# Head pairs on halves of the matrix array, and a router that searches two rows in turn

## The chip, the cores and the metric

The kernel runs on one core of a Trainium2 chip. The metric is the device time of one execution in microseconds (us). TensorE (PE in the profile, its weight loads PEld) multiplies, VectorE (DVE) and ScalarE (ACT) work elementwise and reduce, GpSimd (POOL) helps with a few elementwise jobs, and SyncE (SP) issues the transfers that bring weights from HBM.

## The reference, cut to what matters

One sequence of 256 rows and width 1024 goes through a pool mixer, a feed-forward block, chunk attention, a second feed-forward block, a block with two branches (retention and stick-breaking attention), and PEER, an expert layer. Four pieces matter here.

```python
# chunk attention, 16 heads of 64 (scores q.k, bias, mask, softmax, values)
s = jnp.einsum('bqhd,bkhd->bhqk', qc, kb) * scale + bias[None]
p = jax.nn.softmax(jnp.where(valid, s, -1e30), axis=-1)
o = jnp.einsum('bhqk,bkhd->bqhd', p, vb)          # then o @ w_o
# stick-breaking, 8 heads of 64
z = jnp.einsum('bhtd,bhsd->bhts', qi, kh) * scale
later = lax.cumsum(log_stay, axis=3, reverse=True) - log_stay
w = jnp.where(mask, jnp.exp(jax.nn.log_sigmoid(z) + later), 0.0)
out = jnp.einsum('bhts,bhsd->bhtd', w, vh)
# retention, 8 heads with q and k of 64, v of 128
scores = jnp.einsum('bihd,bjhd->bhij', qc, kc) * dmask[None]
# PEER: 16 of 128 sub-keys twice, then 16 of their 256 sums, for each row and head
v1, i1 = lax.top_k(s1, 16); v2, i2 = lax.top_k(s2, 16)
top_s, pos = lax.top_k(v1[..., :, None] + v2[..., None, :], 16)
a = gelu(u_tab[idx] @ x) * softmax(top_s)         # and y = sum of a * v_tab[idx]
```

## The kernel before, in words

All activations stay on the chip; rows are two blocks (b = 0, 1) of 128 partitions. Weights stream from HBM as slabs. Each slab is split into a rounded high part (`whi`, ScalarE, L72) and the rest (`wlo`, VectorE, L80 or L86, a few on GpSimd), and `mm3` (L107 to L111) makes each product of three matmuls. Outside PEER, a planner orders the instructions of each engine from estimated costs, and so fills TensorE with projections (`acc`) while heads wait for other engines. PSUM has four `acc` tiles, three `w` tiles and one `o` tile; `w` tiles are handed out in program order.

**Attention** (`attention`, L443). `qkv(g)` projects eight heads, `heads(g, h0)` works on four of them, head by head: `weights` (scores of 64 rows of the array by L480 and L481, bias L484, maxima L486, exponentials L487 with their sums), `turn` (three transposes L494 and a copy L496) and `values` (L501 to L503: the stationary operand is the turned weights, 128 by 128, the moving one v, 64 columns). After four heads the sum's reciprocal (L515) scales the `o` tile (L517), and `transposed` (L206) turns it again into `oT`, the operand of `out_proj`. Attention calls `heads` four times; the projection of the second half of the heads, and then `out_proj`, lie around them.

**Stick-breaking** (L577) has the same shape: `stay` (L606, L607 and five elementwise instructions), `weights` (L622 to L630), `values` (L636 to L638), a copy and four transposes for four heads. Its two calls are placed between the projections of **retention** (L661), whose `heads` computes scores by L709 and L710 one head at a time.

**PEER** (`peer`, L747) is ordered by hand for TensorE, VectorE and ScalarE. In eight steps `h` it projects the queries (`qps`, L793), computes sub-key scores (`scores`, L968), and in steps 1 and 2 transposes the normalized input into `hn` through `w` and `o` tiles (L801). Then 128 expert slabs follow: `up(i)` (L822, 24 matmuls into `hps`) needs `whi` and `wlo` of slab i. The **router** (`route`, L983) is a generator: each step issues some VectorE work and yields its cost in units; `side(rout, upto)` runs it until the units spent reach `upto`. In step h that is `5 h`, and in the slab loop

```python
for i in range(N1):
    self.prefetch(3, later=True)          # whi of slab i + 2 on ScalarE
    if not side(rout, 36 + i * 1.6):      # router's work on VectorE
        last = i; break
    self.lows()                           # wlo of slab i + 2 on VectorE
    up(i)
```

so that VectorE runs two slabs ahead of TensorE, behind the router's steps. `top16` (L1083) finds 16 maxima of a row by five instructions, each of which needs the one before (MAX8, FIND_INDEX8, MATCH_REPLACE8, MAX8, FIND_INDEX8; the match ones are preceded by a MATCH_VALUE_LOAD). It runs 32 times on 128 columns and 16 times on 64. When the router is done (slab `last`), one-hot matrices for 64 groups of four rows are spread over the other slabs, and the second half of PEER follows.

Of the kernel before, what the change touches and what calls it, by code (L numbers as in the profile page):

```python
# [8 lines left out]
F32 = mybir.dt.float32  # L9
# [4 lines left out]
AF = mybir.ActivationFunctionType  # L14
OP = mybir.AluOpType
# [4 lines left out]
S = 256  # L20
# [26 lines left out]
class K:  # L47
# [158 lines left out]
    def transposed(self, hi, lo, src, b, kts, gcol=None, k0=0):  # L206
# [236 lines left out]
    def attention(self):  # L443
# [27 lines left out]
        def heads(g, h0):  # L471

            o = self.ps.tile([128, 2, 4, 64], F32, tag="o", name="o_ps", bufs=1)
            rs = self.small.tile([128, 2, 4], F32, tag="rsum", name="rsum")
            ss, ps = {}, {}

            def weights(h):
                p, hs = h // 2, slice((h % 2) * 64, (h % 2) * 64 + 64)
                sc = self.ps.tile([128, 384], F32, tag="w", name="sc", bufs=self.nw)
                nc.tensor.matmul(sc[:, 0:128], qT[g][hs, p, 0:128], kT[g][hs, p, 0:128], start=True, stop=True)  # L480
                nc.tensor.matmul(sc[:, 128:384], qT[g][hs, p, 128:256], kT[g][hs, p, :], start=True, stop=True)  # L481
                s = ss[h] = self.stage.tile([128, 384], F32, tag="s", name="s", bufs=3)
                m = self.small.tile([128, 2], F32, tag="mx", name="mx")
                nc.vector.tensor_tensor(s, sc, bias[g][:, h, :], op=OP.add)  # L484
                for b, c in ((0, slice(0, 128)), (1, slice(128, 384))):
                    nc.vector.tensor_reduce(m[:, b:b + 1], s[:, c], axis=AX.X, op=OP.max, negate=True)  # L486
                    nc.scalar.activation(s[:, c], s[:, c], AF.Exp, bias=m[:, b:b + 1],  # L487
                                         accum_out=rs[:, b, h - h0:h - h0 + 1])

            def turn(h):  # L490
                pt = self.ps.tile([128, 3, 128], F32, tag="w", name="pt_ps", bufs=self.nw)
                s = ss.pop(h)
                for j in range(3):
                    nc.tensor.transpose(pt[:, j], s[:, j * 128:(j + 1) * 128], self.ident)  # L494
                ps[h] = self.stage.tile([128, 3, 128], F32, tag="pT", name="pT", bufs=2)
                nc.scalar.activation(ps[h], pt, AF.Copy)  # L496

            def values(h):
                pT = ps.pop(h)
                v = [vv[g][:, b, h * 64:(h + 1) * 64] for b in range(2)]  # L500
                nc.tensor.matmul(o[:, 0, h - h0], pT[:, 0], v[0], start=True, stop=True)  # L501
                nc.tensor.matmul(o[:, 1, h - h0], pT[:, 1], v[0], start=True, stop=False)
                nc.tensor.matmul(o[:, 1, h - h0], pT[:, 2], v[1], start=False, stop=True)  # L503

            weights(h0)
            weights(h0 + 1)
            turn(h0)
            for h in range(h0, h0 + 4):
                if h + 2 < h0 + 4:
                    weights(h + 2)  # L510
                if h + 1 < h0 + 4:
                    turn(h + 1)
                values(h)
            ri = self.small.tile([128, 2, 4], F32, tag="rinv", name="rinv")
            nc.vector.reciprocal(ri, rs)  # L515
            on = self.stage.tile([128, 2, 4, 64], F32, tag="on", name="on", bufs=2)
            nc.vector.tensor_tensor(on.rearrange("p b h d -> p (b h) d"), o.rearrange("p b h d -> p (b h) d"),  # L517
                                    ri.rearrange("p b h -> p (b h)")[:, :, None].to_broadcast([128, 8, 64]),
                                    op=OP.mult)
            for b in range(2):  # L520
                self.transposed(oT[0], oT[1], on[:, b].rearrange("p h d -> p (h d)"), b, 2,
                                k0=g * 4 + h0 // 2)

        qkv(0)
        heads(0, 0)
        heads(0, 4)
        qkv(1)
        heads(1, 0)
        heads(1, 4)
        self.out_proj(lambda k: (oT[0][:, k], oT[1][:, k]))  # L530

# [45 lines left out]
    def stick_breaking(self, hT, r):  # L577
# [19 lines left out]
        def heads(h0):  # L597
            if h0 == 0:
                self.tc.keep_in_program_order(nc.scalar.preload_act_table_set("natural_log_exp_and_others"))
            o = self.ps.tile([128, 2, 4, 64], F32, tag="o", name="sbo", bufs=1)  # L600
            logs = {}

            def stay(h):
                p, hs = h // 2, slice((h % 2) * 64, (h % 2) * 64 + 64)
                z = self.ps.tile([128, 384], F32, tag="w", name="z", bufs=self.nw)
                nc.tensor.matmul(z[:, 0:256], kT[hs, p, 0:128], qT[hs, p, :], start=True, stop=True)  # L606
                nc.tensor.matmul(z[:, 256:384], kT[hs, p, 128:256], qT[hs, p, 128:256], start=True, stop=True)  # L607
                a = st.tile([128, 384], F32, tag="sb_a", name="sb_a", bufs=3)
                sp = st.tile([128, 384], F32, tag="sb_sp", name="sb_sp", bufs=3)
                logs[h] = a, sp  # L610
                nc.scalar.activation(a, z, AF.Abs)
                nc.scalar.activation(a, a, AF.Exp, scale=-1.0)
                nc.scalar.activation(a, a, AF.Ln, bias=1.0)
                nc.vector.scalar_tensor_tensor(sp, z, 0.0, a, op0=OP.max, op1=OP.add)
                nc.vector.scalar_tensor_tensor(a, z, 0.0, a, op0=OP.min, op1=OP.subtract)
                for c in (0, 256):
                    self.strictly_before(sp[:, c:c + 128])

            def weights(h):
                a, sp = logs[h]  # L620
                lt = self.ps.tile([128, 384], F32, tag="w", name="lt", bufs=self.nw)
                nc.tensor.matmul(lt[:, 0:256], self.tri, sp[:, 0:256], start=True, stop=False,  # L622
                                 skip_group_check=True)
                nc.tensor.matmul(lt[:, 128:256], self.ones, sp[:, 256:384], start=False, stop=True,
                                 skip_group_check=True)
                nc.tensor.matmul(lt[:, 256:384], self.tri, sp[:, 256:384], start=True, stop=True,
                                 skip_group_check=True)
                nc.vector.tensor_tensor(a, a, lt, op=OP.subtract)
                nc.scalar.activation(a, a, AF.Exp)
                for c in (0, 256):  # L630
                    self.strictly_before(a[:, c:c + 128])

            def values(h):
                a, _ = logs.pop(h)
                vh = [v[:, b, h * 64:(h + 1) * 64] for b in range(2)]
                nc.tensor.matmul(o[:, 0, h - h0], a[:, 0:128], vh[0], start=True, stop=True)  # L636
                nc.tensor.matmul(o[:, 1, h - h0], a[:, 128:256], vh[0], start=True, stop=False)
                nc.tensor.matmul(o[:, 1, h - h0], a[:, 256:384], vh[1], start=False, stop=True)  # L638

            stay(h0)  # L640
            for h in range(h0, h0 + 4):
                if h + 1 < h0 + 4:
                    stay(h + 1)
                weights(h)
                if h > h0:
                    values(h - 1)
            values(h0 + 3)
            on = st.tile([128, 2, 4, 64], F32, tag="yn", name="sbn", bufs=2)
            nc.scalar.activation(on, o, AF.Copy)
            for b in range(2):  # L650
                self.transposed(yT[0], yT[1], on[:, b].rearrange("p h d -> p (h d)"), b, 2, k0=h0 // 2)

        self.later = [lambda: heads(0), lambda: heads(4)]
# [7 lines left out]
    def retention(self, hT, r):  # L661
# [38 lines left out]
        def heads(h0):  # L700
            sc = st.tile([128, 4, 384], F32, tag="rsc", name="rsc", bufs=1)
            for j in range(4):
                h = h0 + j
                if j % 2 == 0:
                    dec = st.tile([128, 2, 384], F32, tag="dec", name="dec", bufs=1)
                    nc.sync.dma_start(dec, self.ins["c_decay"][:, h:h + 2])
                p, hs = h // 2, slice((h % 2) * 64, (h % 2) * 64 + 64)
                ps = self.ps.tile([128, 384], F32, tag="w", name="rs", bufs=self.nw)
                nc.tensor.matmul(ps[:, 0:256], kT[hs, p, 0:128], qT[hs, p, :], start=True, stop=True)  # L709
                nc.tensor.matmul(ps[:, 256:384], kT[hs, p, 128:256], qT[hs, p, 128:256], start=True, stop=True)  # L710
# [541 lines left out]
```

## Time and profile before

| | |
|---|---|
| median of 3 runs | 1604.07 us (1604.07 to 1605.76) |
| profiled execution | 1604.23 us, span 1602.5 us |
| mean granted TensorE clock | 0.995 |
| TensorE busy | 1565.4 us, 98% |
| TensorE weight loads busy | 1401.5 us, 87% |
| VectorE busy | 1160.3 us, 72% |
| ScalarE busy | 843.0 us, 53% |
| GpSimd busy | 105.0 us, 7% |

The span runs from the first to the last instruction of the program; 1.7 us of the execution lie around it. Busy shares are means over stages; matmuls are pipelined and their ends are modelled, so two matmuls overlap in the record, and the distance from start to start is what one costs the engine. A matmul of plain float32 operands shows as two records.

### The profile page before, as it was taken

What the parts mean: (1) busy time and instruction counts of PE and PEld (TensorE: products, weight loads), DVE (VectorE), ACT (ScalarE), POOL (GpSimd) and SP (SyncE); (2) the same over time, 40 slices, a digit from 0 to 9 for tenths busy, and PEclk for the clock granted to TensorE, in tenths of its full rate; (3) what the DMA queues carried; (4) which work ended last, traced back from release to release, by engine and by line L of the source; (5) the groups of instructions that cost most, each with busy time, mean ns of one, the idle gap of its engine ahead of it and who ended that gap; (6) DMA issues with size and microseconds to landing.
All of it is one profiled execution on the core that took longest, in us unless ns stands there. A gap on an engine that the chain in (4) does not pass through costs nothing.

```text
span 1602.5 us, 26447 instructions
## 1 busy us (share of the span) xinstructions
PE 1565.4 (98%) x10190; PEld 1401.5 (87%) x10190; DVE 1160.3 (72%) x2479; ACT 843.0 (53%) x1563; POOL 105.0 (7%) x111
## 2 busy tenths in 40 slices
PE   5999999999999999999999999999999999999999
PEld 4999987779999887888898999999999888888887
DVE  7676777767767877675599987788888655555554
ACT  6555565565555647444554555454444544454453
POOL 5000020010000202000260000000000000000000
PEclk9999999999999999999999999999999999999999
DMA  5555464325555552455424555555555666666664
GB/s 218 181 196 198 168 237 175 132 83 192 201 183 201 187 183 106 152 178 200 167 76 136 167 174 169 170 171 159 170 161 170 186 197 196 189 194 196 194 192 152
DMA packets 58446, 278.66 MB, mean 174 GB/s; under 512 B 6480, under 2 KB 7376, under 8 KB 41680
## 3 DMA queue, kind: packets, MB, share of 16 engines
q1 hardware_dynamic: 58320, 276.97, 52.6%
q8 instruction: 80, 1.31, 0.3%
q14 instruction: 46, 0.38, 0.1%
HBM read 275.90 MB, written 1.05 MB: 173 GB/s over the span
## 4 chain that ended last, share of the span: by engine, by line
PE 87%; DVE 9%; issue 2%; ACT 1%; DMA 1%; POOL 0%; SPq 0%; DVEq 0%; ACTq 0%; POOLq 0%
PE acc L110 15%; PE acc L111 15%; PE acc L109 15%; PE hps L109 6%; PE hps L111 6%; PE hps L110 6%; PE up L110 5%; PE up L111 5%; PE up L109 5%; PE gps L869 2%; DVE wlo L86 1%; DVE wlo L80 1%; DVE topk L1088 1%; DVE ix L1087 1%; DVE ix L1090 1%
## 5 line engine op out<-in xcount | busy, mean ns | idle before, releaser
L72 ACT ACTIVATE whi<-raw 128x512 fp32r<-128x512 f32 (+1 forms) x764 | 556.3, 769 | 381.3 <-PE acc L111 158.4
L80 DVE TENSOR_TENSOR wlo<-raw,whi 128x512 fp32r<-128x512 f32 (+1 forms) x572 | 448.6, 812 | 137.7 <-ACT whi L72 137.5
L111 PE MATMUL hps<-hn,wlo 128*128 128x256 f32 x1024 | 289.2, 282 | 8.6 <-DVE wlo L86 8.5
L109 PE MATMUL hps<-hn,whi 128*128 128x256 f32 x1024 | 293.5, 287 | 0.0
L110 PE MATMUL hps<-hn,whi 128*128 128x256 f32 x1024 | 287.1, 280 | 0.0
L111 PEld LDWEIGHTS hps<-hn,wlo 128*128 128x128 f32 x1024 | 194.0, 189 | 10.7 <-DVE wlo L86 10.6
L110 PE MATMUL up<-hT,whi 128*128 128x256 f32 x704 | 197.8, 281 | 1.5 <-DVE hT L223 1.5
L109 PE MATMUL up<-hT,whi 128*128 128x256 f32 x704 | 198.1, 281 | 0.4 <-DVE hT L223 0.4
L111 PE MATMUL up<-hT,wlo 128*128 128x256 f32 x704 | 197.4, 280 | 0.0
L110 PE MATMUL acc<-wlo,hn 128*128 128x512 f32 x504 | 196.2, 389 | 0.0
L111 PE MATMUL acc<-whi,hn 128*128 128x512 f32 x504 | 196.2, 389 | 0.0
L109 PE MATMUL acc<-whi,hn 128*128 128x512 f32 x504 | 196.2, 389 | 0.0
L110 PEld LDWEIGHTS hps<-hn,whi 128*128 128x128 f32 x1024 | 194.5, 190 | 0.0
L109 PEld LDWEIGHTS hps<-hn,whi 128*128 128x128 f32 x1024 | 194.3, 190 | 0.0
L86 DVE TENSOR_TENSOR wlo<-raw,whi 128x1024 fp32r<-128x1024 f32 x128 | 155.8, 1219 | 14.8 <-ACT whi L72 14.1
L110 PEld LDWEIGHTS up<-hT,whi 128*128 128x128 f32 x704 | 133.6, 190 | 3.3 <-DVE hT L223 2.0
L109 PEld LDWEIGHTS up<-hT,whi 128*128 128x128 f32 x704 | 133.5, 190 | 2.1 <-issue 0.7
L111 PEld LDWEIGHTS up<-hT,wlo 128*128 128x128 f32 x704 | 133.6, 190 | 0.0
L110 PE MATMUL acc<-wlo,hT 128*128 128x512 f32 (+1 forms) x320 | 125.0, 391 | 2.2 <-DVE wlo L80 1.2
L80 POOL TENSOR_TENSOR wlo<-raw,whi 128x512 fp32r<-128x512 f32 x64 | 84.3, 1347 | 636.0 <-ACT whi L72 629.3
L111 PE MATMUL acc<-whi,hT 128*128 128x512 f32 (+1 forms) x320 | 124.7, 390 | 0.0
L109 PE MATMUL acc<-whi,hT 128*128 128x512 f32 (+1 forms) x320 | 124.4, 390 | 0.0
(291 smaller groups left out, 2486.1 us busy)
## 6 DMA issues: line engine op xcount, KB each, us to landing
raw<-in_peer_u SPq DMA_DIRECT2D x128, 512.0 KB, 3.6
raw<-in_peer_v SPq DMA_DIRECT2D x128, 512.0 KB, 3.6
raw<-in_wup SPq DMA_DIRECT2D x44, 1024.0 KB, 4.9
raw<-in_win SPq DMA_DIRECT2D x26, 1024.0 KB, 4.8
raw<-in_wdn SPq DMA_DIRECT2D x22, 1024.0 KB, 4.8
raw<-in_wqkv SPq DMA_DIRECT2D x12, 1024.0 KB, 4.9
raw<-in_wo SPq DMA_DIRECT2D x8, 1024.0 KB, 4.8
raw<-in_peer_wq SPq DMA_DIRECT2D x8, 1024.0 KB, 4.8
```

The costliest lines, as they stand in the source:

```text
L72: i = nc.scalar.activation(hi[:, c:c + n], raw[:, c:c + n], AF.Copy)
L80: low(*args, op=OP.subtract)
L86: self.nc.vector.tensor_tensor(*self.low_parts.pop(0), op=OP.subtract)
L109: mm(ps, lh, rh, start=start, stop=False)
L110: mm(ps, lh, rl, start=False, stop=False)
L111: mm(ps, ll, rh, start=False, stop=stop)
L869: nc.tensor.matmul(ps[:, j], jh[:, j], gh[:, n, j], start=n == 0, stop=n == 1)
L1087: nc.vector.max_index(out=ix[:, 0:8], in_max=v[:, 0:8], in_values=s)
L1088: nc.vector.match_replace(out=t, in_to_replace=v[:, 0:8], in_values=s, imm_value=-3.0e38)
L1090: nc.vector.max_index(out=ix[:, 8:16], in_max=v[:, 8:16], in_values=t)
```

## The change

Heads are handled in pairs. The two heads of a pair lie on partitions 0 to 63 and 64 to 127 of the same q and k tile, so that their score matmuls use the two row halves of the array; the change issues them one behind the other. The values are computed transposed: v (64 columns) is the stationary operand, the weights the moving one, and the two heads write the two partition halves of one `o` tile of 128 by 256. So `oT` comes out of `split` directly; in attention the weights are normalized before they are turned. In the router, `top16` takes two rows and issues each of its five steps for both, and yields after the second step too; `unstair` is cut into three steps; some unit costs and the slope (1.6 to 1.5) change. The transposes of PEER's input go through `acc` tiles.

```diff
-            tag, bufs = ("o", 1) if kts == KT and b == 1 and k == 4 else ("w", self.nw)
+            tag, bufs = bank or (("o", 1) if kts == KT and b == 1 and k == 4 else ("w", self.nw))
...
-        def heads(g, h0):
+        def heads(g, pairs):
...
+            def weights(p):
+                sc = [self.ps.tile([128, 384], F32, tag="w", name="sc", bufs=self.nw) for _ in range(2)]
+                hs = [slice(e * 64, e * 64 + 64) for e in range(2)]
+                for e in range(2):
+                    nc.tensor.matmul(sc[e][:, 0:128], qT[g][hs[e], p, 0:128], kT[g][hs[e], p, 0:128],
+                                     start=True, stop=True)
+                for e in range(2):
+                    nc.tensor.matmul(sc[e][:, 128:384], qT[g][hs[e], p, 128:256], kT[g][hs[e], p, :],
+                                     start=True, stop=True)
+                s = ss[p] = self.stage.tile([128, 2, 384], F32, tag="s", name="s", bufs=2)
...
+                for e in range(2):
+                    nc.vector.tensor_tensor(s[:, e], sc[e], bias[g][:, 2 * p + e, :], op=OP.add)
+                    for b, c in parts:
+                        nc.vector.tensor_reduce(m[:, e, b:b + 1], s[:, e, c], axis=AX.X, op=OP.max, negate=True)
+                        nc.scalar.activation(s[:, e, c], s[:, e, c], AF.Exp, bias=m[:, e, b:b + 1],
+                                             accum_out=rs[:, e, b:b + 1])
+                nc.vector.reciprocal(ri, rs)
+                for e in range(2):
+                    for b, c in parts:
+                        nc.vector.tensor_scalar(s[:, e, c], s[:, e, c], ri[:, e, b:b + 1], None, op0=OP.mult)
...
+            def values(p):
+                pT = ps.pop(p)
+                o = self.ps.tile([128, S], F32, tag="o", name="o_ps", bufs=1)
+                self.head_values(o, [vv[g][:, b, p * 128:(p + 1) * 128] for b in range(2)],
+                                 [pT[:, e].rearrange("p j t -> p (j t)") for e in range(2)])
+                self.split(oT[0][:, g * 4 + p], oT[1][:, g * 4 + p], o)
+            last = None
+            for p in pairs:
+                weights(p)
+                if last is not None:
+                    values(last)
+                turn(p)
+                last = p
+            values(last)
...
+    def head_values(self, o, v, w):
+        mm = self.nc.tensor.matmul
+        for b in range(2):
+            for e in range(2):
+                hs = slice(e * 64, e * 64 + 64)
+                t = slice(b * 128, S)
+                c = slice(0, 256) if b == 0 else slice(256, 384)
+                mm(o[hs, t], v[b][:, hs], w[e][:, c], start=b == 0, stop=b == 1, skip_group_check=True)
...
-                    self.transposed(*hT, xn.pop(0), h - 1, KT, V_FFN2)
+                    self.transposed(*hT, xn.pop(0), h - 1, KT, V_FFN2, bank=("acc", 4))
...
-                if not side(rout, 36 + i * 1.6):
+                if not side(rout, 36 + i * 1.5):
...
+    def top16(self, rt, cost, rows):
+        vec = self.nc.vector
+        t = [rt.tile([128, 128], F32, tag="topk", name="topk", bufs=4)[:, :s.shape[1]] for _, _, s in rows]
+        for v, _, s in rows:
+            vec.max(out=v[:, 0:8], in_=s)
+        for v, ix, s in rows:
+            vec.max_index(out=ix[:, 0:8], in_max=v[:, 0:8], in_values=s)
+        yield cost
+        for (v, _, s), r in zip(rows, t):
+            vec.match_replace(out=r, in_to_replace=v[:, 0:8], in_values=s, imm_value=-3.0e38)
+        for (v, _, s), r in zip(rows, t):
+            vec.max(out=v[:, 8:16], in_=r)
+        for (v, ix, s), r in zip(rows, t):
+            vec.max_index(out=ix[:, 8:16], in_max=v[:, 8:16], in_values=r)
+        yield cost
```

Stick-breaking is rewritten in the same way (`stay`, `weights` and `values` of a pair), with four `sb_a` tiles for three and without the copy of `o`. Retention's `heads` issues the score matmuls of two heads together and then their two products with the decay. In `route`, a row of 128 columns still costs 1.2 units and one of 64 columns 0.9, `unstair` costs 3.7 in three steps for 2.4 in one, the last step of the selection 1.9 for 1.4, and the `sc` tiles are four for five.

## Rows read from the trace of the kernel before

**Rows 1.** Stages: stretch, length, busy us (count) of PE, PEld, DVE, ACT, POOL, clock, DMA.

```profile
840.80:946.80 106.00, 97.42 (x785) 95.34 (x784) 98.31 (x319) 52.00 (x63) 0.00 (x0) 0.97 0.50 155
946.80:1247.00 300.20, 300.20 (x2792) 297.47 (x2791) 250.23 (x488) 148.96 (x294) 0.00 (x0) 1.00 0.55 169
314.00:355.40 41.40, 41.05 (x227) 31.35 (x226) 27.32 (x69) 25.33 (x77) 1.73 (x2) 1.00 0.26 98
```

**Rows 2.** Waits, whole span: who waited for whom, us in total, times, longest.

```profile
PEld hps L111 <- DVE wlo L86: 10.6, 10, 2.8
```

**Rows 3.** Timeline of PE, slab loop: start, length, line, operation [idle before it].

```profile
849.78 0.38 PE L111 MATMUL hps<-hn,wlo 128*128 128x256 f32 x1 [1.98 <-DVE wlo L86]
...
851.33 0.42 PE L109 MATMUL hps<-hn,whi 128*128 128x256 f32 x1
...
922.38 0.28 PE L109 MATMUL hps<-hn,whi 128*128 128x256 f32 x1
...
925.18 0.28 PE L109 MATMUL hps<-hn,whi 128*128 128x256 f32 x1
```

**Rows 4.** Timeline of DVE: one search of 128 columns, and the next one's start.

```profile
839.09 0.29 DVE L1086 MAX8 v<-scores 128x8 f32<-128x128 f32 x1
839.41 0.09 DVE L1087 MATCH_VALUE_LOAD ix<-v,scores 128x8 f32 x1
839.49 0.28 DVE L1087 FIND_INDEX8 ix<-v,scores 128x8 uint32<-128x128 f32 x1
839.69 0.07 DVE L1088 MATCH_VALUE_LOAD topk<-v,scores 128x8 f32 x1
...
840.67 0.28 DVE L1086 MAX8 v<-scores 128x8 f32<-128x128 f32 x1
```

**Rows 5.** Timeline of DVE: a slab's low part, then a search of 64 columns.

```profile
864.68 1.22 DVE L86 TENSOR_TENSOR wlo<-raw,whi 128x1024 fp32r<-128x1024 f32 x1
865.81 0.22 DVE L1086 MAX8 top<-cand 128x8 f32<-128x64 f32 x1
...
867.06 1.21 DVE L86 TENSOR_TENSOR wlo<-raw,whi 128x1024 fp32r<-128x1024 f32 x1
```

**Rows 6.** Timeline, PEER's step 1 to 2: transposes of the input, then the next projection.

```profile
797.65 1.04 PE L215 MATMUL pt<-ident,hn 128*128 128x128 f32 x8
...
800.94 0.39 PE L109 MATMUL qps<-hT,whi 128*128 128x256 f32 x1 [2.25 <-DVE hn L223]
```

**Rows 7.** Timeline of PE, stick-breaking: scores of one head, then of two heads together.

```profile
609.18 0.70 PE L606 MATMUL z<-sbT 64*128 64x256 f32 x2
...
610.03 0.70 PE L622 MATMUL lt<-sb_sp,tri 128*128 128x256 f32 x2
...
625.82 0.71 PE L606 MATMUL z<-sbT 64*128 64x256 f32 x4
...
626.68 0.50 PE L110 MATMUL acc<-wlo,hT 128*128 128x512 f32 x1
627.02 0.39 PE L111 MATMUL acc<-whi,hT 128*128 128x512 f32 x1
627.25 0.40 PE L109 MATMUL acc<-whi,hT 128*128 128x512 f32 x1
```

**Rows 8.** Timeline of PE, attention's last four heads.

```profile
328.21 0.49 PE L480 MATMUL sc<-qkT 64*128 64x128 f32 x2
...
332.30 0.27 PE L494 MATMUL pt_ps<-ident,s 128*128 128x128 f32 x1
...
334.70 0.39 PE L502 MATMUL o_ps<-vv,pT 128*128 128x64 f32 x2
334.92 0.39 PE L503 MATMUL o_ps<-vv,pT 128*128 128x64 f32 x2
...
341.44 0.62 PE L215 MATMUL pt<-ident,on 128*128 128x128 f32 x4
```

**Rows 9.** The tile xn: line, count, shortest, median, longest ns.

```profile
L304 DVE TENSOR_SCALAR xn<-x,rms x4: 479/484/489, 7.9 to 14.8; 128x512 f32<-128x512 f32 x4
```

More of the change, by code (lines that the diff above doesn't have):

```diff
@@ L204, in split, with transposed @@
             nc.vector.scalar_tensor_tensor(lo, src, g, hi.bitcast(F32), op0=OP.mult, op1=OP.subtract)
-    def transposed(self, hi, lo, src, b, kts, gcol=None, k0=0):
+    def transposed(self, hi, lo, src, b, kts, gcol=None, k0=0, bank=None):
         nc = self.nc
@@ L469, in qkv @@
                     qn = self.head_norm(ps, r)
-        def heads(g, h0):
-            o = self.ps.tile([128, 2, 4, 64], F32, tag="o", name="o_ps", bufs=1)
-            rs = self.small.tile([128, 2, 4], F32, tag="rsum", name="rsum")
+        def heads(g, pairs):
             ss, ps = {}, {}
[L477 to L522, printed above, removed]
@@ new lines, in weights @@
+            def weights(p):
[8 more added lines that the diff above has]
+                s = ss[p] = self.stage.tile([128, 2, 384], F32, tag="s", name="s", bufs=2)
+                m = self.small.tile([128, 2, 2], F32, tag="mx", name="mx")
+                rs = self.small.tile([128, 2, 2], F32, tag="rsum", name="rsum")
+                ri = self.small.tile([128, 2, 2], F32, tag="rinv", name="rinv")
+                parts = (0, slice(0, 128)), (1, slice(128, 384))
+                for e in range(2):
[8 more added lines that the diff above has]
+                        nc.vector.tensor_scalar(s[:, e, c], s[:, e, c], ri[:, e, b:b + 1], None, op0=OP.mult)
@@ new lines, in turn @@
+            def turn(p):
+                s = ss.pop(p)
+                ps[p] = self.stage.tile([128, 2, 3, 128], F32, tag="pT", name="pT", bufs=2)
+                for e in range(2):
+                    pt = self.ps.tile([128, 3, 128], F32, tag="w", name="pt_ps", bufs=self.nw)
+                    for j in range(3):
+                        nc.tensor.transpose(pt[:, j], s[:, e, j * 128:(j + 1) * 128], self.ident)
+                    nc.scalar.activation(ps[p][:, e], pt, AF.Copy)
+            def values(p):
[4 more added lines that the diff above has]
+                self.split(oT[0][:, g * 4 + p], oT[1][:, g * 4 + p], o)
@@ L524, in attention @@
+            last = None
[6 more added lines that the diff above has]
+            values(last)
         qkv(0)
-        heads(0, 0)
-        heads(0, 4)
+        heads(0, (0, 1))
+        heads(0, (2, 3))
         qkv(1)
-        heads(1, 0)
-        heads(1, 4)
+        heads(1, (0, 1))
+        heads(1, (2, 3))
         self.out_proj(lambda k: (oT[0][:, k], oT[1][:, k]))
+    def head_values(self, o, v, w):
+        mm = self.nc.tensor.matmul
+        for b in range(2):
+            for e in range(2):
+                hs = slice(e * 64, e * 64 + 64)
+                t = slice(b * 128, S)
+                c = slice(0, 256) if b == 0 else slice(256, 384)
+                mm(o[hs, t], v[b][:, hs], w[e][:, c], start=b == 0, stop=b == 1, skip_group_check=True)
@@ L595, in stick_breaking, with heads @@
         self.later = []
-        def heads(h0):
-            if h0 == 0:
+        def heads(pairs):
+            if 0 in pairs:
                 self.tc.keep_in_program_order(nc.scalar.preload_act_table_set("natural_log_exp_and_others"))
-            o = self.ps.tile([128, 2, 4, 64], F32, tag="o", name="sbo", bufs=1)
             logs = {}
[L603 to L651, printed above, removed]
@@ L653, in stick_breaking, with stay @@
-        self.later = [lambda: heads(0), lambda: heads(4)]
+            def stay(p):
+                z = [self.ps.tile([128, 384], F32, tag="w", name="z", bufs=self.nw) for _ in range(2)]
+                hs = [slice(e * 64, e * 64 + 64) for e in range(2)]
+                for e in range(2):
+                    nc.tensor.matmul(z[e][:, 0:256], kT[hs[e], p, 0:128], qT[hs[e], p, :], start=True, stop=True)
+                for e in range(2):
+                    nc.tensor.matmul(z[e][:, 256:384], kT[hs[e], p, 128:256], qT[hs[e], p, 128:256],
+                                     start=True, stop=True)
+                logs[p] = []
+                for e in range(2):
+                    a = st.tile([128, 384], F32, tag="sb_a", name="sb_a", bufs=4)
+                    sp = st.tile([128, 384], F32, tag="sb_sp", name="sb_sp", bufs=3)
+                    logs[p].append((a, sp))
+                    nc.scalar.activation(a, z[e], AF.Abs)
+                    nc.scalar.activation(a, a, AF.Exp, scale=-1.0)
+                    nc.scalar.activation(a, a, AF.Ln, bias=1.0)
+                    nc.vector.scalar_tensor_tensor(sp, z[e], 0.0, a, op0=OP.max, op1=OP.add)
+                    nc.vector.scalar_tensor_tensor(a, z[e], 0.0, a, op0=OP.min, op1=OP.subtract)
+                    for c in (0, 256):
+                        self.strictly_before(sp[:, c:c + 128])
@@ new lines, in weights @@
+            def weights(p):
+                for a, sp in logs[p]:
+                    lt = self.ps.tile([128, 384], F32, tag="w", name="lt", bufs=self.nw)
+                    nc.tensor.matmul(lt[:, 0:256], self.tri, sp[:, 0:256], start=True, stop=False,
+                                     skip_group_check=True)
+                    nc.tensor.matmul(lt[:, 128:256], self.ones, sp[:, 256:384], start=False, stop=True,
+                                     skip_group_check=True)
+                    nc.tensor.matmul(lt[:, 256:384], self.tri, sp[:, 256:384], start=True, stop=True,
+                                     skip_group_check=True)
+                    nc.vector.tensor_tensor(a, a, lt, op=OP.subtract)
+                    nc.scalar.activation(a, a, AF.Exp)
+                    for c in (0, 256):
+                        self.strictly_before(a[:, c:c + 128])
@@ new lines, in values @@
+            def values(p):
+                o = self.ps.tile([128, S], F32, tag="o", name="sbo", bufs=1)
+                self.head_values(o, [v[:, b, p * 128:(p + 1) * 128] for b in range(2)],
+                                 [a for a, _ in logs.pop(p)])
+                self.split(yT[0][:, p], yT[1][:, p], o)
+            last = None
+            for p in pairs:
+                stay(p)
+                if last is not None:
+                    values(last)
+                weights(p)
+                last = p
@@ L654, in stick_breaking @@
+            values(last)
+        self.later = [lambda: heads((0, 1)), lambda: heads((2, 3))]
         return yT
@@ L701, in heads @@
             sc = st.tile([128, 4, 384], F32, tag="rsc", name="rsc", bufs=1)
-            for j in range(4):
+            for j in range(0, 4, 2):
                 h = h0 + j
[L704 to L710, printed above, removed]
-                nc.vector.tensor_tensor(sc[:, j], ps, dec[:, j % 2], op=OP.mult)
+                dec = st.tile([128, 2, 384], F32, tag="dec", name="dec", bufs=1)
+                nc.sync.dma_start(dec, self.ins["c_decay"][:, h:h + 2])
+                p, hs = h // 2, [slice(e * 64, e * 64 + 64) for e in range(2)]
+                ps = [self.ps.tile([128, 384], F32, tag="w", name="rs", bufs=self.nw) for _ in range(2)]
+                for e in range(2):
+                    nc.tensor.matmul(ps[e][:, 0:256], kT[hs[e], p, 0:128], qT[hs[e], p, :], start=True, stop=True)
+                for e in range(2):
+                    nc.tensor.matmul(ps[e][:, 256:384], kT[hs[e], p, 128:256], qT[hs[e], p, 128:256],
+                                     start=True, stop=True)
+                for e in range(2):
+                    nc.vector.tensor_tensor(sc[:, j + e], ps[e], dec[:, e], op=OP.mult)
             v = rv[h0 // 4]
@@ L977, in scores @@
                                  start=True, stop=True)
-        sc = rt.tile([128, 2, 2, 128], F32, tag="sc", name="scores", bufs=5)
+        sc = rt.tile([128, 2, 2, 128], F32, tag="sc", name="scores", bufs=4)
         for b in range(2):
@@ L995, in route @@
             for b in range(2):
-                for s in range(2):
-                    self.top16(rt, v[:, b, 2 * h + s], ix[:, b, 2 * h + s], self.sc[h][:, b, s])
-                    yield 1.2
+                yield from self.top16(rt, 1.2, [(v[:, b, 2 * h + s], ix[:, b, 2 * h + s], self.sc[h][:, b, s])
+                                                for s in range(2)])
         for b in range(2):
@@ L1012, in route @@
             yield 1.3
-            for h in range(8):
-                self.top16(rt, top[:, h], code[:, 2, h], cand[:, h])
-                yield 0.9
+            for h in range(0, 8, 2):
+                yield from self.top16(rt, 0.9, [(top[:, i], code[:, 2, i], cand[:, i]) for i in (h, h + 1)])
             abf = rt.tile([128, 2, 8 * TOPK, 2], F16, tag="abf", name="abf", bufs=1)
-            self.unstair(rt, abf, code)
-            yield 2.4
+            yield from self.unstair(rt, abf, code)
             sel = rt.tile([128, 3, 8, TOPK], F32, tag="sel", name="sel", bufs=1)
@@ L1081, in unstair @@
         nc.vector.tensor_tensor(ab[:, 1], flat(c[:, 2]), flat(f), op=OP.subtract)
-    def top16(self, rt, v, ix, s):
-        nc = self.nc
-        t = rt.tile([128, 128], F32, tag="topk", name="topk", bufs=2)[:, :s.shape[1]]
-        nc.vector.max(out=v[:, 0:8], in_=s)
-        nc.vector.max_index(out=ix[:, 0:8], in_max=v[:, 0:8], in_values=s)
-        nc.vector.match_replace(out=t, in_to_replace=v[:, 0:8], in_values=s, imm_value=-3.0e38)
-        nc.vector.max(out=v[:, 8:16], in_=t)
-        nc.vector.max_index(out=ix[:, 8:16], in_max=v[:, 8:16], in_values=t)
+        yield 1.4
+    def top16(self, rt, cost, rows):
[13 more added lines that the diff above has]
+        yield cost
     def finish(self):
```

8 lines of the change are left out of this document (5 added, 3 removed).

## The prediction

> **What bounds the kernel now.** I read the page first: TensorE is busy 98% of the span at full clock nearly everywhere, VectorE 72%. So nothing but TensorE's own time counts, unless another engine makes it wait. Next I read the windows by stage, to see where that is not so [rows 1]. In the second half of attention TensorE is busy for 41.05 of 41.40 us: time is gained there by fewer or shorter matmuls alone. In the router's slab loop it is busy for 97.42 of 106 us while VectorE is busy for 98.31: VectorE sets the pace there. In the 300 us after it VectorE is busy 250 us and TensorE never idle.
>
> Then the waits and the timeline of the slab loop. TensorE waits 10.6 us in ten waits for `wlo` [rows 2]; the reader should see in [rows 3] that after the wait of 1.98 us at slab 2 the same matmul takes 0.42 us for 0.28: TensorE has dropped to the lower of its two clock levels for a while, and the mean clock of the window is 0.97 [rows 1]. What the loop loses in all: an undisturbed slab of 24 matmuls takes 922.38 to 925.18, 2.80 us [rows 3]; the window's 785 records are 32 slabs (768) and 17 small ones of about 0.1, together 91.3 us. The rest, 106.0 - 91.3 = 14.7 us, is lost: 10.6 by waits, about 4 by the clock and the refilling behind them.
>
> **The change, part by part.** *The router's searches.* In [rows 4] a search takes 839.09 to 840.67, 1.58 us. MAX8 is followed 0.32 later, its result being needed; FIND_INDEX8, equally long, is followed 0.20 later by an instruction that needs nothing of it. Two rows in turn put an independent instruction behind each: per row two MAX8 at 0.20, two index steps at 0.28 (load 0.08 and find 0.20), and one replacement at 0.26 (load 0.06, and 0.20 taken for it as for the others of 128 columns): 1.22 us. On 64 columns 865.81 to 867.06 is 1.25 us [rows 5]; with the same three waits gone (0.12 each) about 0.90. Slab by slab VectorE also makes a low part, 864.68 to 865.81, 1.13 us [rows 5]. Before, 1.6 units at 1.58 us for 1.2 units are 2.11, with 1.13 makes 3.24 us per slab against TensorE's 2.80: it falls behind. After, 1.5 / 1.2 x 1.22 = 1.53, and 1.5 / 0.9 x 0.90 = 1.50 for the short rows, with 1.13 at most 2.66 us: it keeps up. The new unit costs only charge `unstair` and the selection with about what they take, so that no step runs far past its allowance. Slab 2 was late since by the units six searches (four of step 7, two of slab 0) lie ahead of its low part; they get 6 x 0.36 = 2.2 us shorter, against a wait of 1.98 [rows 3]. Bounds: 0 (VectorE still late) to 14.7; I take 14. The loop ends later (units 38.4 + 2 x 22.3 = 83 for 78.4, at 1.5 for 1.6 per slab: some five slabs), so the 64 one-hot groups crowd into 88 slabs for 93; VectorE is idle for 50 us of 300 there [rows 1], and covers that.
>
> A rule of the Trainium skill speaks against this step (VectorE: DVE Perf Modes, section The DRAIN you can't avoid): the next instruction starts when the pipe has emptied, with or without a semaphore between. By it two rows in turn would gain nothing; the trace differs, 0.20 behind an independent instruction against 0.32 [rows 4].
>
> *The input's transposes through `acc` tiles.* The projection of step 2 waits 2.25 us until VectorE has read a `w` tile [rows 6]. The four `acc` tiles are free between the steps, so the wait goes: 2.3 us, bounds 0 and 2.3. ScalarE and VectorE still turn the tile into `hn`, hidden under the next projections.
>
> *Scores in pairs.* One head's scores take 609.18 to 610.03, 0.85 us; two heads that happen to lie one behind the other take 625.82 to 626.68, 0.86 us [rows 7]. So row halves do run side by side already, wherever the planner put two heads together: in the timeline 6 pairs of 16 stand so (two in attention, two in stick-breaking, two in retention), 20 heads stand alone. Pairing all of these saves 10 x 0.84 = 8.4 us. But the second head of a pair needs a second of three `w` tiles, which comes free only when ScalarE has copied a turned one: the planner can put other matmuls between, as it did before. Bounds 0 and 8.4; I take 5.
>
> *Values, transposed.* Before, each of three matmuls costs 334.70 to 334.92, 0.22 us [rows 8], 0.66 per head, 15.8 for 24 heads; and four transposes for each four heads at (0.62 - 0.27) / 3 = 0.12 [rows 8], 2.8 us for 24: 18.6 us go. After, each half of a pair moves 256 and 128 columns, which are the sizes of a head's scores: 0.85 us if the two column halves run side by side as row halves do, 12 pairs 10.2 us; if they run one after the other, 0.64 more (0.85 less about 0.1 each for entering and leaving the halves, by the 0.34 for 0.23 behind a pair in [rows 7]), 17.9. No row shows column halves: the gain is between 0.7 and 8.4. Row halves being the nearest, I take them as side by side, less 0.7 for pairs whose second half comes late: 7.7.
>
> The Trainium skill (TensorE: Matmul & The Clock Gate, Part 3) has three column tiles run 2.38 times as fast as one after the other, not three; by that two halves would save some 2 us less, an estimate that no row here shows. Its page TensorEngine Tiling (Array Packing), Key Properties, says that a change of tiling mode drains the array: the trace agrees, the first projection behind a pair takes 0.34 us to the next start, then 0.23 [rows 7].
>
> *What is added.* Four multiplications of 128 or 256 columns per pair on VectorE, each under the 0.48 us of 512 columns [rows 9], less a multiplication of 512 per four heads. VectorE is busy 27 of 41 us there [rows 1], so its work is hidden, but it lengthens the chain from scores to values. From 328.21 to 332.30 two heads' softmax took 4.1 us [rows 8]; with a reciprocal and four multiplications about 5.3, with six transposes (0.7) and a copy (0.5) 6.5 per pair, before the next pair has both tiles. Four pairs: 26 us. TensorE has, beside them, 4 x (0.85 + 0.85 + 0.7) = 9.6 us of heads and the first 48 `out_proj` matmuls at 0.23 [rows 7], 11: 20.6. Up to 6 us are uncovered unless the planner pulls up the 24 matmuls (5.5 us) of the pairs already done. Bounds 0 and 7; I take 3.5 lost. In the first half and in stick-breaking two or more projections of 11 us each cover it.
>
> **Sum.** 14 + 2.3 + 5 + 7.7 - 3.5 = 25.5 us off the profiled 1604.2 (0.2 us from the median): 1578.7, say 1579.
>
> **Rivals.** *Column halves run one after the other*: 7.7 back, 1586. For it: no row shows them side by side. Against: row halves do it.
> *The pairs fall apart* and the chain is uncovered: scores gain nothing (5 back), the stall is 7 (3.5 more): 1587. For it: three `w` tiles, 20 heads alone before. Against: both heads of a pair become ready nearly together.
> *The search gains nothing by turns* (the drain, after every VectorE instruction alike): 1.5 / 1.2 x 1.58 + 1.13 = 3.1 us per slab, 0.3 too much over 37 slabs, 11 us back: 1590. The rule of the DRAIN section named above would do this. Against it: [rows 4].
> *Slower*: TensorE runs out of other work at the pairs. If each of 12 pairs leaves it idle for 2 us, the clock falls behind it as in [rows 3] and costs 2 more: 48 us lost for the 3.5, 1623. It decides from 2.4 us per pair on ((25.5 + 3.5) / 12). For it: the chain of 6.5 us per pair, with one pair in flight. Against: outside attention's end some 11 us of projections lie beside each call.
> *The change does not do what it says*: heads were paired already where it counted, column halves are serial, VectorE's relief ends in waits for ScalarE, which makes `whi`; each gain goes: 1604. Against: ScalarE is busy 52 of 106 us there [rows 1].
>
> **How the numbers follow.** A measurement of this kernel tells about 0.2% (3.2 us) from no change. Chances: forecast 0.56, serial columns 0.14, pairs apart 0.14, search 0.07, slower 0.05, no effect 0.04. The forecast's own range is 1570 (all pairs, no stall: 3.4 + 3.5 better, and 2 for visits saved) to 1585. The range takes in the next three rivals up to 1590 and leaves out the last two: 1569 to 1591. Faster 0.91, same 0.04, slower 0.05.
>
> **What would show it.** Right: no wait for `wlo` over 1 us in the slab loop and a clock of 1.00 there; a search of two rows in about 2.45 us; `o_ps` matmuls of the two halves starting within some 20 ns, a pair in about 0.9 us; `sc` matmuls in groups of eight. Wrong: `o_ps` halves 0.2 us or more apart in turn, single heads' `sc` groups with `acc` between, TensorE idle behind `s` or `pT` between 290 and 350 us, or waits on `wlo` that go on past slab 3.

## The result, and the profile after

The change takes 1576.86 us (median of 4 runs, 1575.42 to 1577.07) for 1604.07, a ratio of 0.9826 with a 95% interval of 0.9813 to 0.9838. The prediction was 1579 (1569 to 1591). The profiled execution took 1575.42 us, its span is 1573.7. Each experiment below was timed beside the kernel before, whose median was 1604.5 to 1605.2 us there; ratios and gains over the kernel before are against that. So a difference of about 1 us between two kernels timed apart says little by itself, and the stages of the traces are read with it.

Where the time went is read from the starts of TensorE's first matmul of each stage in the two timelines (us):

| stage | before | after | difference | predicted |
|---|---|---|---|---|
| up to attention's first projection | 225.7 | 223.3 | -2.4 | 0 |
| attention | 129.7 | 122.7 | -7.0 | -9.2 with the branches |
| second feed-forward block | 187.0 | 187.2 | +0.2 | 0 |
| the two branches and their mixing | 242.3 | 240.0 | -2.3 | see attention |
| query steps | 56.1 | 53.8 | -2.4 | -2.3 |
| first to last `up` of the slabs | 409.3 | 394.3 | -15.0 | -14 |
| the rest | 352.4 | 352.4 | 0 | 0 |

The first row is no effect of the change: TensorE's order is the same there, and of the twelve other profiles of this study one reaches attention at 224.1, the others between 224.6 and 226.2. The other rows add up to 26.5 us, for 25.5 predicted.

The windows of the router's slab loop and of the second half of attention, as in [rows 1] and with the same columns:

```profile
827.00:933.00 106.00, 106.00 (x912) 106.00 (x911) 96.20 (x319) 59.15 (x71) 0.00 (x0) 1.00 0.58 180
308.00:346.00 38.00, 37.57 (x205) 27.45 (x203) 28.24 (x77) 25.00 (x76) 1.80 (x2) 1.00 0.30 108
```

In the router's slab loop TensorE is now busy for all of 106 us, at a clock of 1.00, and does 912 matmuls where it did 785; VectorE has about as much to do as before. The wait of [rows 2] is in no line of the list of waits any more. In the second half of attention TensorE is as busy as before, for 38.0 us instead of 41.4.

VectorE's timeline shows the search in turn; to be read against [rows 4, 5]:

```profile
827.23 0.47 DVE L1102 MAX8 v<-scores 128x8 f32<-128x128 f32 x2
...
829.57 0.47 DVE L1102 MAX8 v<-scores 128x8 f32<-128x128 f32 x2
...
897.04 0.33 DVE L1102 MAX8 top<-cand 128x8 f32<-128x64 f32 x2
...
897.69 1.21 DVE L86 TENSOR_TENSOR wlo<-raw,whi 128x1024 fp32r<-128x1024 f32 x1
898.81 0.08 DVE L1107 MATCH_VALUE_LOAD topk<-top,cand 128x8 f32 x1
...
899.87 0.33 DVE L1102 MAX8 top<-cand 128x8 f32<-128x64 f32 x2
```

Two MAX8 take 0.39 us to the next start (827.62), where one that is followed by an instruction in need of it took 0.32. Two rows of 128 columns take 2.34 us, 1.17 for one where it was 1.58. Two of 64 columns take 0.65 and, behind a slab's low part, 1.06: 0.86 for one, where it was 1.25.

The wait of [rows 6] is gone too; the projection starts as soon as the transposes are issued:

```profile
786.29 1.04 PE L215 MATMUL pt<-ident,hn 128*128 128x128 f32 x8
787.08 0.37 PE L109 MATMUL qps<-hT,whi 128*128 128x256 f32 x1
```

TensorE's timeline of the values of two pairs in attention and of the scores of one pair in stick-breaking, for [rows 7, 8]:

```profile
316.76 0.87 PE L542 MATMUL o_ps<-pT,vv 128*64 128x256 f32 x8
317.56 0.50 PE L110 MATMUL acc<-wlo,oTh 128*128 128x512 f32 x1
...
335.54 0.65 PE L542 MATMUL o_ps<-pT,vv 128*64 128x256 f32 x2
336.11 0.49 PE L111 MATMUL acc<-whi,oTl 128*128 128x512 f32 x1
336.54 0.86 PE L542 MATMUL o_ps<-pT,vv 128*64 128x256 f32 x6
337.33 0.50 PE L109 MATMUL acc<-whi,oTh 128*128 128x512 f32 x1
...
593.26 0.70 PE L618 MATMUL z<-sbT 64*128 64x256 f32 x4
593.79 0.39 PE L620 MATMUL z<-sbT 64*128 64x128 f32 x4
594.11 0.50 PE L110 MATMUL acc<-wlo,hT 128*128 128x512 f32 x1
```

The first pair's eight values records stand together: 0.80 us to the next start, its two halves starting 6 to 7 ns apart. The second pair has come apart: two records, a projection, six records, 0.57 and 0.79 us. The scores of stick-breaking stand together, 0.85 us. What the engine spends on each kind, summed from the timelines as the distance from each matmul's start to the next matmul's (us; a wait counts with the matmul ahead of it):

```
                             before   after   late_head_first
scores: attention  sc         12.9     10.6      10.6
  stick-breaking   z           5.5      3.4       3.4
  retention        rs          5.0      5.0       5.0
values: attention  o_ps       10.8      8.1       6.4
  its transposes   on          1.8      0         0
  stick-breaking   sbo         5.4      6.6       4.0
  its transposes   sbn         0.8      0         0
```

### The profile page after: what moved, and what is told of

Same layout as the page of the kernel before. It is cut to its first block, busy times and chain, and to the rows that moved or that the text cites. A ratio compares the mean times of both kernels' runs of the same rounds, so it can differ in the third digit from the quotient of the medians.

```text
span 1573.7 us, 26320 instructions
## 1 busy us (share of the span) xinstructions
PE 1547.3 (98%) x10118; PEld 1383.2 (88%) x10118; DVE 1148.4 (73%) x2510; ACT 839.9 (53%) x1557; POOL 105.9 (7%) x111
## 4 chain that ended last, share of the span: by engine, by line
PE 92%; DVE 2%; POOL 2%; issue 2%; ACT 1%; DMA 1%; SPq 0%; POOLq 0%; ACTq 0%; DVEq 0%
PE acc L111 15%; PE acc L110 15%; PE acc L109 15%; PE hps L109 8%; PE hps L111 8%; PE hps L110 8%; PE up L110 5%; PE up L111 5%; PE up L109 5%; PE gps L883 2%; POOL wlo L80 1%; PE qps L110 1%; PE qps L111 1%; PE qps L109 1%; DMA raw<-in_wup 1%
```

## The experiments

**The router.** Four kernels. `router_only` is the kernel before with the router's hunks alone (slope, `sc` tiles, `route`, `unstair`, `top16`).

> The kernel before with the router's edits alone (two rows in turn, finer steps, unit costs, slope 1.5, four score tiles for five). Theory A, the parts add up: the start of the expert slabs to their last one fell by 15.0 us between the two traces, so 1604.1 - 15 = 1589, no wait for wlo over 1 us in the slab loop, and the query steps keep their 56 us. Theory B, part of the 15 us came from the other edits (VectorE relieved by the transposes, other times of arrival): the gain is under 12, 1592 or more, and waits for wlo are left.

Measured: 1589.85 us, 0.9908 (0.9893 to 0.9923) of before, 15.0 us less. The slabs from first to last `up` take 394.25 us, to the hundredth what they take with the whole change, and no wait for `wlo` is left. Theory A.

`one_row_each` takes the turns back and nothing else (the lines added; they stand for the body of `top16` in the change):

```diff
+        for (v, ix, s), r in zip(rows, t):
+            vec.max(out=v[:, 0:8], in_=s)
+            vec.max_index(out=ix[:, 0:8], in_max=v[:, 0:8], in_values=s)
+            vec.match_replace(out=r, in_to_replace=v[:, 0:8], in_values=s, imm_value=-3.0e38)
+            vec.max(out=v[:, 8:16], in_=r)
+            vec.max_index(out=ix[:, 8:16], in_max=v[:, 8:16], in_values=r)
+            yield cost
```

> The changed kernel with the five steps of a search issued for one row after the other again; as many yields of the same cost, the same slope. Theory A, the turns make VectorE keep up: a slab's work there is again 1.5 / 1.2 x 1.58 + 1.13 = 3.1 us against 2.80 on TensorE, 0.3 too much over some 37 slabs, 9 to 13 us more than 1577, so 1586 to 1590, with waits for wlo. Theory B, the finer steps, costs and the slope do it: 1577, within 2 us.

Measured: 1586.07 us, 9.2 more than the change; the slabs take 402.5, 8.3 more. Its list of waits:

```profile
PEld hps L111 <- DVE wlo L86: 6.8, 6, 3.1
```

Theory A: one search of 128 columns takes 1.58 us again, and TensorE waits for the low parts again, less than before the change (10.6, [rows 2]).

`coarse_steps` keeps the turns and takes the finer steps back (`yield 2 * cost` at the end of a pair of rows only, `yield 3.7` at the end of `unstair`).

> The changed kernel with the searches still in turn, but with one yield of the whole cost behind a pair of rows and one behind unstair. Theory A, two slabs' lead covers a step of 2.34 us as it covers one of half its length, and only the sum per slab counts: 1577, within 1.5 us, no wait for wlo over 1 us. Theory B, the finer steps are needed: a slab's low part that waits behind a whole pair comes late, waits for wlo of 0.5 to 2 us at several slabs, 1579 to 1585.

Measured: 1578.84 us, 2.0 more; the slabs take 395.9, 1.7 more. In its list of waits:

```profile
PEld hps L111 <- DVE wlo L86: 1.1, 2, 0.6
```

Neither as stated: two low parts come late, by 0.5 to 0.6 us each. So the lead of two slabs covers nearly all of a long step.

`slope_16` has `36 + i * 1.6` again.

> The changed kernel with the router's old allowance of 1.6 units per slab in the slab loop. Theory A, the turns alone make room: by the measured 2.34 us for two rows a slab's work is 1.6 / 1.2 x 1.17 + 1.13 = 2.69 us for TensorE's 2.80, so VectorE keeps up: 1577, within 1 us. Theory B, the lower allowance is needed as well, since single slabs get up to half a pair too much and the lead of two slabs isn't built up at the start: waits for wlo in the first slabs, 1 to 4 us more, 1578 to 1581.

Measured: 1577.51 us, the slabs 394.4. Theory A: beside the turns the slope gives nothing that shows.

**The transposes.** `bank_undone` calls `transposed` without `bank=("acc", 4)`.

> The changed kernel with the transposes of PEER's input through w and o tiles again. Theory A, the wait of 2.25 us for VectorE comes back in the query steps and nowhere else: 1576.9 + 2.4 = 1579.2. Theory B, a later start of the slabs gives the router that much more time, or the wait was hidden elsewhere: 1577, within 1 us.

Measured: 1581.27 us (1578.91 to 1582.27), 4.4 more; the query steps take 57.7 us for 53.8. That is 1.6 more than in the kernel before, whose wait is equally long (2.5 us in both). The windows around the wait, first of `bank_undone`, then of the kernel before (columns as above, the clock before the last two):

```profile
789.00:792.00 3.00, 0.75 (x6) 0.51 (x5) 1.64 (x7) 3.00 (x11) 0.04 (x1) 1.00 0.94 300
792.00:796.00 4.00, 4.00 (x23) 4.00 (x22) 4.00 (x28) 1.92 (x4) 4.00 (x4) 0.57 0.09 37
```

```profile
798.00:801.20 3.20, 0.95 (x9) 0.71 (x8) 1.45 (x6) 3.20 (x12) 0.00 (x0) 1.00 0.66 236
801.20:805.00 3.80, 3.80 (x34) 3.80 (x34) 3.60 (x20) 2.12 (x5) 3.65 (x3) 1.00 0.19 80
```

The reader is to see the clock behind the wait: 0.57, near the lower of its two levels, in the one, and 1.00 in the other. The wait came back and nowhere else, as theory A has it, but its price is 2.4 us in one trace and 4.0 in the other. The four times of `bank_undone` suggest that one kernel can pay either, three being 1581.1 to 1582.3 and one 1578.91; with one of them profiled, that isn't shown.

**The heads.** `heads_only` is the kernel before with the head pairs alone.

> The kernel before with the head pairs alone (attention, stick-breaking, retention); router and transposes as before. Theory A, the parts are independent: attention gave 7.0 us and the two branches 2.3 between the traces, 1604.6 - 9.3 = 1595.3, and the slab loop waits for wlo as before. Theory B, the slab loop's loss depends on when it begins or on the transposes: more than 2.5 us off that.

Measured: 1598.02 us, 0.9958 (0.9943 to 0.9973), 6.5 us less and not 9.3: theory B, by a small margin. Attention and the branches take the 122.7 and 240.1 us that they take with the whole change. The loss lies behind them: the query steps take 57.7 us for 56.1 and the slabs 410.7 for 409.3. The window behind the wait in the query steps, at a clock of 0.67, and the waits in the slabs:

```profile
792.30:796.30 4.00, 3.86 (x22) 3.87 (x23) 3.79 (x21) 2.51 (x5) 3.45 (x3) 0.67 0.25 104
...
PEld hps L111 <- DVE wlo L86: 13.4, 13, 2.8
```

`late_head_first` exchanges the two heads in `head_values`:

```diff
         for b in range(2):
-            for e in range(2):
+            for e in (1, 0):
```

> The changed kernel with the two heads of the values matmuls in the other order, the head whose weights are ready last first. Theory A, seven of the twelve pairs come apart because the first head's matmul is issued alone as soon as its weights are there: all twelve then stand side by side at 0.80 us, 9.6 us for the 14.7 that they take now; of the 5 saved about 1 is a wait that stays: 1572 to 1573. Theory B, a pair that waits for its second head only moves TensorE's work about: 1577, within 1 us.

Measured: 1573.60 us, 0.9804 (0.9791 to 0.9818) of before, 3.3 less than the change. By stages it is 2.3 in attention and 0.9 in the branches; the table above shows `o_ps` at 6.4, eight times 0.80, and `sbo` at 4.0. Theory A, a little short of its size: the values take 4.3 us less, of which the stages keep 3.2. In the branches, by the same count, the projections take 205.0 us for 202.7; part of that is a longer wait for GpSimd's last piece of `sb_a` ahead of a pair (1.9 us in three waits for 0.9 in two). The pair that stood apart at 335.54 is whole:

```profile
336.49 0.87 PE L542 MATMUL o_ps<-pT,vv 128*64 128x256 f32 x8
337.30 0.50 PE L111 MATMUL acc<-whi,oTl 128*128 128x512 f32 x1
```

`head_by_head` exchanges the loops as well (`for e in (1, 0)` outside, `for b in range(2)` inside).

> late_head_first with the loops of the values matmuls exchanged: both matmuls of one head, then both of the other. Theory A, the column halves work side by side only where their matmuls stand next to each other: the inner two of four still do in part, the outer two run alone, 1.07 to 1.3 us for a pair where it is 0.80: 12 pairs cost 3 to 6 us more than late_head_first's 1573.6, so 1576.5 to 1579.5. Theory B, column halves share nothing and a pair's 0.80 us is its own length in any order: 1573.6, within 1 us.

Measured: 1576.82 us, 3.2 more than `late_head_first`. But a pair in attention takes 0.80 to 0.81 as before, and only stick-breaking is slower; the branches take 241.1 us for 239.2, and the two traces don't place the rest of the 3.2:

```profile
290.02 0.88 PE L542 MATMUL o_ps<-pT,vv 128*64 128x256 f32 x8
290.82 0.50 PE L109 MATMUL acc<-whi,hT 128*128 128x512 f32 x1
...
601.92 1.57 PE L542 MATMUL sbo<-sb_a,sv 128*64 128x256 f32 x8
603.41 0.50 PE L110 MATMUL acc<-wlo,hT 128*128 128x512 f32 x1
```

In the pair at 290.02 the second head's 256-column matmul starts 13 ns behind the first head's, although the first head's 128-column matmul stands between them in the program. So the half that is free seems to take its next matmul past one that queues for the other. A rival is that the planner, which orders these matmuls, put the two wide ones side by side. Against it: where they do follow one another, in `late_head_first`, they start 6 to 7 ns apart in all eight pairs, here 12 to 14, as in the scores of the kernel before at 625.82 ([rows 7]), which are also written head by head. In the pair at 601.92 the first head's second matmul waits for GpSimd, which writes the last piece of `sb_a`, and the other head's matmuls wait behind it: 1.49 us. Theory A failed for attention (order alone costs nothing there); that the time lies in its range is due to stick-breaking and another reason, the wait in the queue.

`late_and_pinned` and `second_in_o` try to keep the scores together as well, both from `late_head_first`: the first ties the four score matmuls of a pair in the planner's order, in attention and in retention; the second ties them in attention and takes the second head's tile from the `o` bank.

```diff
-                for e in range(2):
-                    nc.tensor.matmul(sc[e][:, 0:128], qT[g][hs[e], p, 0:128], kT[g][hs[e], p, 0:128],
-                                     start=True, stop=True)
...
+                for c in (0, 128):
+                    for e in (1, 0):
+                        i = nc.tensor.matmul(sc[e][:, c:c + 128 + c], qT[g][hs[e], p, c:c + 128],
+                                             kT[g][hs[e], p, 0:128 + c], start=True, stop=True)
+                        if c or not e:
+                            self.tc.keep_in_program_order(i)
```

> late_head_first, and the score matmuls of a pair in attention and retention tied one behind the other in the planner's order. Theory A, scores in attention still come apart in five of eight pairs because the planner issues one head as soon as one w tile is free (10.6 us for the eight pairs, where eight at 0.86 would be 6.9): tied, at least the wider matmuls of a pair stand together, 1.5 to 3 us less than late_head_first, 1571 to 1572. Theory B, a tied pair makes TensorE wait for the second tile and gives the gain back: 1573.6, within 1 us, and idle time before sc matmuls.

> late_head_first, with the score tile of a pair's second head in attention taken from the o tile's bank instead of a third w tile, and the score matmuls tied in the planner's order. Theory A, the pairs of scores in attention come apart for want of a w tile (10.6 us for eight pairs, where late_and_pinned, tied alone, still took 10.2): with a bank of its own the second head need not wait for a w tile, the wider matmuls stand together in all eight pairs and the shorter ones in half of them, 7.5 to 9 us, and 1.5 to 3 us come off late_head_first's 1573.6: 1570.6 to 1572. Theory B, the o tile, which the values need as well, becomes what the pairs wait for; heads come later and visits of TensorE to the halves get more: 1573.6 to 1576.

Measured: 1573.46 us for `late_and_pinned`, `sc` 10.2 for 10.6: theory A failed; retention's scores fall from 5.0 to 4.5. For B its list of waits has 1.0 us before `sc`, in three waits for ScalarE's copy of a turned tile, where that of `late_head_first` has none. `second_in_o` took 1576.08 us, 2.5 more than `late_head_first`; `sc` falls to 9.1, so a bank did stand in the way, but attention as a whole takes 0.7 us more and the feed-forward block 0.8: a loss, theory B.

`no_normalise` drops `reciprocal` and the `tensor_scalar` loop in attention's `weights`.

> The changed kernel without the reciprocals and the four multiplications that normalize a pair's weights in attention (these are left out of the computation). Theory A, the longer chain from scores to values is covered by the projections: 1576 to 1577, no change over 1 us. Theory B, the prediction's term: the chain costs 3.5 us, and without these five instructions, some 1.2 us of the 6.5 per pair, 1 to 3.5 us come back, 1573 to 1575.5.

Measured: 1579.29 us, 2.4 more than the change, 1.8 of it in attention. Nothing comes back, so theory B isn't borne out. But the run does not isolate the chain: with other times the planner puts the heads elsewhere, and `sc` takes 12.4 us for 10.6, about what attention lost. How TensorE's work falls matters more here than the chain's length.

## Why the prediction was right

**The router's searches: right, and the turns for the reason given.** Predicted 14, measured 15.0, by the router's part alone. Two rows take 2.34 us (2.45 predicted), 64 columns 0.86 (0.90), and the router ends about slab 37 for 32, the five slabs later that were predicted. Without the turns 8.3 of the 15.0 are lost. The other 6.7 come from the rest and stay undivided: beside the turns the finer steps are worth 1.7, the slope nothing measurable, and the unit costs weren't tried alone. The prediction took a rule that would have made this step gain nothing from the Trainium skill (VectorE: DVE Perf Modes, section The DRAIN you can't avoid: the next instruction waits until the pipe has emptied, semaphore or not). It left out that the same section lets a next operation that is not held start earlier; so the section doesn't speak against the step, and the trace agrees with its exception, 0.20 us behind a MAX8 for 0.32. `one_row_each` against the change is the test of the rival, 9.2 us.

**The transposes: right in size.** Predicted 2.3, measured 2.4 between the traces. That the wait may cost 4.0 us, with the lower clock behind it, was not foreseen.

**Scores in pairs: right in size, 4.4 for 5.** Stick-breaking is wholly paired. In attention the sign named, groups of eight `sc` records side by side, is not seen: two pairs of eight have both matmuls side by side, in two visits, as two had before; of the others most overlap in part. Retention is as before (5.0 us). The prediction named the reason, a second `w` tile that comes late; for attention `second_in_o` bears it out in part (9.1 for 10.6), for retention no run does.

**Values, transposed: the mechanism right, the size wrong.** Predicted 7.7, measured 4.1 (18.8 us before, 14.7 after). Column halves do run side by side, 0.80 us for the 0.85 assumed, so the rival of serial columns is out. But 0.7 was taken off for pairs whose second half comes late, and seven of twelve pairs come apart. `late_head_first` shows the rest: in that order the values take 10.4, a gain of 8.4.

**The chain: the step that failed.** Predicted 3.5 lost, between 0 and 7. In the last 38.0 us TensorE is idle for 0.4, over all of attention for 0.95 us, where it was 0.75: some 0.2 us lost. The prediction named the way out: the planner pulls up the `out_proj` matmuls of pairs already done. By the trace 69 of the 96 start before the last values, 43 before the change; the prediction's 48 and the 24 to be pulled up are 72. It took half of a loss that didn't come.

So the heads' sum was right (9.2 for 9.3) by luck: two errors of 3.6 and 3.5 cancel. What else differs is in no term: the weights' transposes take 0.9 us more, the projections 1.5 less. The rival of the pairs falling apart was half true, and the stall that it adds was not. The heads alone gave 6.5: what a stage gains may be taken back behind it.

**The best version** is `late_head_first`, 1573.60 us; tying the scores adds nothing to it that shows.

## What to carry to other kernels

When two independent streams are to share halves of the array, put the matmul first whose operand is ready last: the other one then follows at once. In the opposite order the early one goes alone. Where a row shows that an instruction is followed sooner if the next needs nothing of it, two chains in turn are worth counting, per slab, against the engine that sets the pace. And check each term of a sum on its own: a right total may hold two wrong ones.

## What the runs showed of the hardware

The halves of the array work side by side: a pair of 256 and 128 columns takes 0.85 us on row halves, as one head alone did, and 0.80 on column halves. In `head_by_head` a matmul for the free half starts 13 ns behind the first, past one that the program has before it for the busy half; the trace doesn't show the queue, so that order is inferred from the 13 ns. A wait on a semaphore still stops all that stands behind it (1.49 us for 0.80). The Trainium skill (TensorEngine Tiling (Array Packing), Key Properties) says that tiles work independently, and the trace agrees. The Trainium skill (TensorE: Matmul & The Clock Gate, Part 3) says that matmuls start strictly in order; if the queue holds the program's order, the trace differs.

Behind the same wait of 2.5 us the granted clock stays at 1.00 in two kernels (before, `router_only`) and falls to 0.57 over 4 us in `bank_undone` and to 0.67 in `heads_only`. The query step's matmuls ahead of it are the same; what decides it stays open.
